# Moving adaLN filler steps along layer 0, and two elementwise steps from VectorE to ScalarE

## The chip, the cores and the metric

One core of one Trainium2 chip. The core has a matrix engine (PE in the profile, its weight loads PEld), a vector engine (DVE), a scalar engine (ACT), a general engine (POOL) and a queue for transfers (SP); they run on their own and wait for each other by semaphores. The metric is the device time of one execution of the kernel in microseconds, the median of several runs, as the slowest core shows it (here there is one).

## The reference, cut to what matters

Two layers are applied to 640 tokens of width 2048: 128 context tokens and 512 latent ones, with the same weights and two conditioning vectors. All data is in 32 bit.

```python
def layer_step(x, cvec, p, rope, attend, s0_f, s0_b):
    shift, scale, gate = adaln(cvec, w_ada, b_ada)       # silu(cvec) @ w_ada + b_ada
    h = rms_norm(x, norm_g) * (1.0 + scale) + shift
    aq, ak, av, ag, bq, bff, bfb, bi, bg, cu, cv, cg = split_proj(h @ w_in)
    q, k, v = qkv_heads(aq, ak, av, qg, kg, rope)
    a_out = attend(q, k, v) * jax.nn.silu(ag)
    b_out, s_f, s_b = hgrn_mixer(bq, bff, bfb, bi, bg, lb, hg, s0_f, s0_b)
    c_out = sgu_mixer(cu, cv, cg, lng, lnb, ws, bs)
    y = jnp.concatenate([a_out, b_out, c_out], axis=-1) @ w_out
    return x + gate * y, k, v, s_f, s_b
```

`w_ada` is 2048 x 6144 a layer: 12 column blocks of 512, of which blocks 0 to 3 give the shift, 4 to 7 the scale and 8 to 11 the gate. `attend` is a windowed softmax attention of 8 heads with a sink in the denominator; `hgrn_mixer` is a recurrence over 4 heads, run forward and backward, whose output is normalised per token and head.

## The kernel before, in words

The tokens stand as five tiles of 128 (the first is the context). Every product with `w_in` and `w_out` is taken in three matmuls on high and low parts (`wsplit`, L635 to 642: ACT rounds the weight into `wh`, DVE subtracts to get `wl`). A pass over 512 columns with tokens as rows is `rowmajor` (240 matmuls, L652 to L654, in 15 groups; the last group takes two weight tiles); a pass over 128 columns with tokens as columns is `colmajor` (96 matmuls, L660, in four groups).

Layer 0 goes through these passes: the first round and the first query pass, the second query pass, BI, CU of heads 1 to 3 and CG of head 0, then for each of four recurrence heads BFF, BFB, BQ and BG, then AG of heads 0 to 5, CV, AG of heads 6 and 7, CG of heads 1 to 3, `split_mix`, and the output projection `out_proj` in four column chunks. Layer 1 begins with `begin_next`: norm, scaling and split of its input (L586 to L624), then four row passes, then the same order, with its CU passes after CV.

Two kinds of other work are woven in. The side queue (`self.side`) holds generators of the attention (`attn`), the recurrence (`hgrn`) and the gating unit (`sgu`), moved on by `tick` at set places in each pass. The filler is a generator of adaLN blocks: each call of `fill`, one a group, adds `fill_rate` to a credit and takes one step for each whole credit.

```python
    def fill(self):
        self.credit += self.fill_rate
        while self.credit >= 1:
            self.credit -= 1
            self.step()
```

A block (`ada_steps`, L290) takes 18 steps. Each of the first 16 loads a 128 x 512 piece of `w_ada` into one of two buffers, on SP, with raised priority, and multiplies and adds it on DVE into the accumulator `aacc`, once for each conditioning vector (L300 for the first piece, L302 for the others). There is one `aacc` buffer. The 17th step is empty; the 18th sums over partitions on PE (L308 for the gate, L319 for shift and scale) and writes the result (`mod_cols`). Layer 0's queue has 12 blocks, set in `begin`: its own gate, then layer 1's shift and scale; layer 1's queue has its own gate, at rate 0.5, set after the first pass of `begin_next`. They are counted here from 0 to 11, and 12 to 15. `drain` takes all steps that are left; it is called after each layer's output projection.

The text below numbers these `fill` calls from the second query pass of layer 0 on: 15 a row pass, 4 a column pass, 169 up to `split_mix`, 60 in the output projection.

The order of instructions on each engine isn't the order of the text: a scheduler makes it, from priorities (the place in the text; `hi()` raises it by 3000) and from when inputs and buffers are free.

In `attn`, scores go through exp on ACT with the row sum as a second output (L925), then DVE adds the sink's term, takes the reciprocal (L927, L928) and multiplies the four heads' probabilities by it (L930); four ticks later PE transposes them (L941). A tile of 128 queries has 512, 384 or, for the context, 128 probabilities a head. In `hgrn`, for each of five tiles PE sums the output in a PSUM bank, ACT squares it with a row sum (L1123) and DVE copies it to `ob` (L1124); at the end DVE scales `ob` (L1137) and PE transposes it (L1143).

In `out_proj`, each chunk takes five PSUM banks; the last CG pass before it must empty its two banks first, which `mul_evac` does (exp on ACT, L1206, product on DVE, L1208, then `sigma`, L226 to L229).

Of the kernel before, what the change touches and what calls it, by code (L numbers as in the profile page):

```python
# [12 lines left out]
AF = mybir.ActivationFunctionType  # L13
ALU = mybir.AluOpType
# [4 lines left out]
P = 128  # L19
# [56 lines left out]
class Net:  # L76
# [788 lines left out]
    def attn(self, l, gi, t):  # L865
        nc = self.nc
# [7 lines left out]
        rmax, nmx, es, den = (st[:, 4 * i:4 * i + 4] for i in range(4))  # L874
        snk = self.snk[:, l, 4 * gi:4 * gi + 4]
        nsnk = self.nsnk[:, l, 4 * gi:4 * gi + 4]
        if t > 0:
# [9 lines left out]
            for h in range(4):  # L887
# [3 lines left out]
                for p0, ds, pn in pieces:  # L891
                    ks = slice(p0, p0 + ds * pn, ds)
                    so = s[:, o * P:(o + pn) * P].rearrange("p (b k) -> p b k", k=P)
                    for i, (x, y) in enumerate(((qh, kh), (qh, kl), (ql, kh))):
# [5 lines left out]
                                               op0=ALU.add, op1=ALU.max, accum_out=rmax[:, h:h + 1])  # L900
# [4 lines left out]
            dst = src  # L905
        else:
# [11 lines left out]
            dst = [m[:, h * P:h * P + P] for h in range(4)]  # L918
# [8 lines left out]
        nc.vector.tensor_tensor(den, den, es, op=ALU.add)  # L927
        nc.vector.reciprocal(den, den)  # L928
        for h in range(4):
            nc.vector.tensor_scalar(dst[h], dst[h], den[:, h:h + 1], None, op0=ALU.mult)  # L930
        yield
        yield
        yield
# [114 lines left out]
    def hgrn(self, l, h, es, q):  # L1048
        nc, I, O = self.nc, self.I, self.O
# [7 lines left out]
        for d in range(2):  # L1057
# [7 lines left out]
            for n in range(4):  # L1065
                j = order[d][n]
# [13 lines left out]
        ob = self.g()  # L1080
        ss = self.small(NT, "oss")

        def build(j):
            K = []
            for d in range(2):
                k = self.Cm[:, d, 0:512]
                dd = pre[d][3][:, j, 0:4]
                if d:
                    dd = dd[:, :, ::-1]
                nc.gpsimd.tensor_tensor(k.rearrange("p (i c s) -> p i c s", i=4, c=4),  # L1090
                                        bc(c4(pre[d][0])[:, j], 1, 4), bc(dd, 3, 32), op=ALU.mult)
                K.append(k)
            return K
# [4 lines left out]
        for n in range(NT + 3):  # L1098
            if n < NT:
                for d in range(2):  # L1100
                    qe = pre[d][1]
                    ab = self.bank()
                    for i in range(4):
                        ri = 3 - i if d else i
                        nc.tensor.matmul(ab[32 * i:32 * i + 32, 0:P], lhsT=qe[:, n * P + 32 * i:n * P + 32 * i + 32],  # L1105
                                         rhs=K[d][:, ri * P:(ri + 1) * P], start=True, stop=True,
                                         skip_group_check=True)
                    nc.vector.copy_predicated(self.att[d], self.m8[:, 1 - d], ab[:, 0:P])
                asum = self.sml.tile([P, P], F32, tag="asum", name=self.nm("asum"), bufs=2)
                nc.vector.tensor_tensor(asum, self.att[0], self.att[1], op=ALU.add)  # L1110
                sums[n] = asum
                if n + 1 < NT:
                    K = build(n + 1)
            if n >= 3:
                j = n - 3
                oo = self.bank()
                nc.tensor.matmul(oo[:, 0:P], lhsT=aTs[j], rhs=vj[j], start=True, stop=j == 0)
                if j > 0:
                    for d in range(2):
                        nc.tensor.matmul(oo[:, 0:P], lhsT=pre[d][2][:, j * P:(j + 1) * P],  # L1120
                                         rhs=S[d][:, order[d].index(j) - 1], start=False, stop=d == 1)
                junk = self.sml.tile([P, P], BF16, tag="junk", name=self.nm("junk"), bufs=1)
                nc.scalar.activation(junk, oo[:, 0:P], AF.Square, accum_out=ss[:, j:j + 1])  # L1123
                nc.vector.tensor_copy(ob[:, j * P:(j + 1) * P], oo[:, 0:P])  # L1124
            yield
            if 1 <= n <= NT:
                tb = self.bank()
                nc.tensor.transpose(tb[:, 0:P], sums.pop(n - 1), self.ident)
                aT = self.sml.tile([P, P], F32, tag="aT", name=self.nm("aT"), bufs=2)
                nc.scalar.activation(aT, tb[:, 0:P], AF.Copy)  # L1130
                aTs[n - 1] = aT
                yield
# [8 lines left out]
        for j in range(NT):  # L1141
            dst = b1[:, j * P:(j + 1) * P] if j < 4 else b2[:, 0:P]
# [128 lines left out]
    def begin(self, W):  # L1271

        with self.hi():
            self.setup()
            self.first_round(W)
            act, dve = self.second_round(W)
        with self.tc.issue_after(act), self.tc.issue_after(dve):
            self.setup2()
            self.prep_ctx(0)
        self.filler = self.ada_gen([(0, b) for b in range(8, 12)] + [(1, b) for b in range(8)])  # L1280
        self.fill_rate = 1.0
        steps = self.bias_rows(W)

        def hook(k):
            if k < 8:
                self.shift_h(k + 8)
            if k:
                next(steps, None)

        ps = self.rowmajor(W, AQ + 512, hook)  # L1290
        for _ in steps:
            pass
        self.q_evac(0, 1, ps)
# [18 lines left out]
    def layer(self, l):  # L1312
        W = self.I["w_in"][l]
        nc = self.nc
# [47 lines left out]
        if l > 0:  # L1362
            self.drain()
        self.split_mix()
        self.out_proj(l)
        self.drain()

# [56 lines left out]
```

## Time and profile before

| what | value |
|---|---|
| median of 3 runs | 2344.2 us (2340.97 to 2345.61) |
| the profiled execution's own time | 2338.18 us |
| its span, from the first to the last instruction | 2336.4 us |
| mean granted clock of PE | 0.988 |
| second query pass to CG of head 0 (layer 0) | 205.7 to 457.5 us |
| recurrence passes, layer 0 | 457.5 to 739.6 us |
| AG, CV, AG and CG passes, layer 0 | 739.6 to 998.9 us |
| output projection, layer 0 | 998.9 to 1247.9 us, with the first part of the hand-over to layer 1 |
| recurrence passes, layer 1 | 1531.6 to 1805.7 us |
| output projection, layer 1 | 2114.0 to 2331.4 us |

The stages run from the first matmul of one pass to the first of the next. In the rows of the profile a line number is that of the kernel; `x480` is a count; after the bar come busy us, mean ns of one, then the engine's idle time ahead of the group and what ended it. A busy PE is no measure by itself, since matmuls overlap; how long the same matmuls take in two stages is.

### The profile page before, as it was taken

What the parts mean: (1) busy time and instruction counts of PE and PEld (TensorE: products, weight loads), DVE (VectorE), ACT (ScalarE), POOL (GpSimd) and SP (SyncE); (2) the same over time, 40 slices, a digit from 0 to 9 for tenths busy, and PEclk for the clock granted to TensorE, in tenths of its full rate; (3) what the DMA queues carried; (4) which work ended last, traced back from release to release, by engine and by line L of the source; (5) the groups of instructions that cost most, each with busy time, mean ns of one, the idle gap of its engine ahead of it and who ended that gap; (6) DMA issues with size and microseconds to landing.
All of it is one profiled execution on the core that took longest, in us unless ns stands there. A gap on an engine that the chain in (4) does not pass through costs nothing.

```text
span 2336.4 us, 34944 instructions
## 1 busy us (share of the span) xinstructions
PE 2261.4 (97%) x13308; PEld 1968.0 (84%) x13308; DVE 1424.3 (61%) x2612; ACT 778.7 (33%) x1605; POOL 293.9 (13%) x234
## 2 busy tenths in 40 slices
PE   7999999999999989989999999999999999999999
PEld 5766678899999888977787878799999998998887
DVE  3436987768887766666667455855875942434223
ACT  3323434343334322332224234344343332223111
POOL 0000111002122211011112010101222220101110
PEclk9999999999999999999999999999999999999999
DMA  9675632434433354355552221322332323324332
GB/s 321 218 254 191 209 117 83 148 95 120 126 117 104 111 163 144 111 192 171 173 170 91 77 68 47 115 68 72 111 94 76 114 90 92 103 75 149 106 106 84
DMA packets 264876, 296.41 MB, mean 127 GB/s; under 512 B 17378, under 2 KB 166772, under 8 KB 262916
## 3 DMA queue, kind: packets, MB, share of 16 engines
q1 hardware_dynamic: 254368, 271.27, 37.2%
q10 hardware_dynamic: 10340, 22.91, 3.2%
q8 instruction: 104, 1.70, 0.3%
q14 instruction: 64, 0.52, 0.1%
HBM read 280.38 MB, written 13.73 MB: 126 GB/s over the span
## 4 chain that ended last, share of the span: by engine, by line
PE 75%; DVE 12%; DMA 7%; issue 2%; ACT 1%; POOL 0%; DVEq 0%; ACTq 0%; POOLq 0%
PE m L660 29%; PE m L652 11%; PE m L653 11%; PE m L654 11%; DMA wa<-in_w_ada_dram 6%; DVE aacc L302 4%; DVE wl L641 2%; PE s L240 2%; PE s L895 1%; PE s L941 1%; PE s L1105 1%; PE s L1072 1%; PE s L953 1%; PE s L954 1%; PE s L319 1%
## 5 line engine op out<-in xcount | busy, mean ns | idle before, releaser
L641 DVE TENSOR_TENSOR wl<-wr,wh 128x512 fp32r<-128x512 f32 (+1 forms) x535 | 401.5, 752 | 575.2 <-ACT wh L640 566.7
L640 ACT ACTIVATE wh<-wr 128x512 fp32r<-128x512 f32 (+1 forms) x535 | 336.1, 629 | 971.0 <-PE m L654 557.2
L652 PE MATMUL m<-wh,hh 128*128 128x512 f32 x1440 | 571.6, 397 | 9.2 <-DVE mg L1208 5.3
L653 PE MATMUL m<-wl,hh 128*128 128x512 f32 x1440 | 568.5, 395 | 3.5 <-DVE wl L641 3.5
L654 PE MATMUL m<-wh,hl 128*128 128x512 f32 x1440 | 565.6, 393 | 0.0
L660 PE MATMUL m<-hh,wh 128*128 128x384 f32 x2016 | 478.1, 317 | 0.0
L660 PE MATMUL m<-hl,wh 128*128 128x384 f32 x2016 | 465.0, 311 | 0.0
L660 PE MATMUL m<-hh,wl 128*128 128x384 f32 x2016 | 464.6, 311 | 0.0
L302 DVE SCALAR_TENSOR_TENSOR aacc<-wa,s,aacc 128x512 f32<-128x512 f32 x480 | 368.6, 801 | 72.9 <-DMA wa<-in_w_ada_dram 72.3
L652 PEld LDWEIGHTS m<-wh,hh 128*128 128x128 f32 x1440 | 272.0, 189 | 84.5 <-issue 10.3
L653 PEld LDWEIGHTS m<-wl,hh 128*128 128x128 f32 x1440 | 272.7, 189 | 64.2 <-DVE wl L641 7.4
L654 PEld LDWEIGHTS m<-wh,hl 128*128 128x128 f32 x1440 | 272.4, 189 | 59.0 <-issue 2.6
L660 PEld LDWEIGHTS m<-hh,wh 128*128 128x128 f32 x2016 | 312.5, 190 | 9.8 <-issue 8.1
L660 PEld LDWEIGHTS m<-hl,wh 128*128 128x128 f32 x2016 | 311.5, 189 | 0.4
L660 PEld LDWEIGHTS m<-hh,wl 128*128 128x128 f32 x2016 | 311.1, 189 | 0.3
L1090 POOL TENSOR_TENSOR mg<-ev,Dt 128x512 f32<-128x512 f32 x80 | 95.7, 1213 | 321.5 <-PE s L1105 107.2
L1260 POOL TENSOR_TENSOR mg<-mg,ev 128x512 f32<-128x512 f32 x30 | 43.9, 1473 | 287.9 <-DVE ev L1258 287.1
L751 POOL TENSOR_TENSOR mg<-g,g 128x256 f32<-128x256 f32 x32 | 32.8, 1047 | 263.8 <-DVE g L749 145.5
L925 ACT ACTIVATE g<-g,st,qs 128x384 f32<-128x384 f32 (+1 forms) x64 | 48.1, 752 | 36.0 <-DVE st L921 36.0
L228 ACT ACTIVATE ev<-ev 128x640 f32<-128x640 f32 x40 | 29.5, 738 | 72.3 <-DVE ev L227 71.2
L945 DVE TENSOR_TENSOR g<-s,g 128x512 fp32r<-128x512 f32 x56 | 38.4, 687 | 24.0 <-ACT g L944 18.1
L1045 POOL TENSOR_TENSOR g<-g,EG 128x512 f32<-128x512 f32 x16 | 22.7, 1416 | 239.4 <-DVE Dt L1030 125.1
(272 smaller groups left out, 1984.6 us busy)
## 6 DMA issues: line engine op xcount, KB each, us to landing
wr<-in_w_in_dram SPq DMA_DIRECT2D x406, 256.0 KB, 2.9
wa<-in_w_ada_dram SPq DMA_DIRECT2D x278, 256.0 KB, 3.0
wr<-in_w_out_dram SPq DMA_DIRECT2D x128, 256.0 KB, 2.9
wa<-in_w_ada_dram SPq DMA_DIRECT2D x16, 1024.0 KB, 6.7
wa<-in_w_in_dram SPq DMA_DIRECT2D x9, 1024.0 KB, 6.5
wa<-in_w_ada_dram SPq DMA_DIRECT2D x44, 128.0 KB, 3.3
mg<-const_xT_dram SPq DMA_DIRECT2D x4, 1280.0 KB, 5.8
x<-mg SPq DMA_DIRECT2D x20, 256.0 KB, 2.1
```

The costliest lines, as they stand in the source:

```text
L240: return self.nc.tensor.matmul(acc[32 * q:32 * q + 32, 0:n], lhsT=lhs[:, kk, :], rhs=rhs, start=kk < 4, stop=kk >= 12, skip_group_check=True)
L302: nc.vector.scalar_tensor_tensor(acc[:, cd], r, sc, acc[:, cd], op0=ALU.mult, op1=ALU.add)
L640: nc.scalar.activation(wh, raw, AF.Copy)
L641: nc.vector.tensor_tensor(wl, raw, wh.bitcast(F32), op=ALU.subtract)
L652: nc.tensor.matmul(ps, lhsT=hh, rhs=wh[:, 0], start=k == 0, stop=False)
L653: nc.tensor.matmul(ps, lhsT=hh, rhs=wl[:, 0], start=False, stop=False)
L654: nc.tensor.matmul(ps, lhsT=hl, rhs=wh[:, 0], start=False, stop=k == KT - 1)
L660: self.nc.tensor.matmul(ps[hf][:, 0:n], lhsT=w[:, a], rhs=h[:, o:o + n], start=k == 0 and i == 0, stop=k == KT - 1 and i == 2)
L925: nc.scalar.activation(dst[h], src[h], AF.Exp, bias=nmx[:, h:h + 1], scale=rq[:, h:h + 1], accum_out=den[:, h:h + 1])
L945: nc.vector.tensor_tensor(pt[1], pb, pt[0].bitcast(F32), op=ALU.subtract)
L1090: nc.gpsimd.tensor_tensor(k.rearrange("p (i c s) -> p i c s", i=4, c=4), bc(c4(pre[d][0])[:, j], 1, 4), bc(dd, 3, 32), op=ALU.mult)
L1260: (nc.vector if c == 3 else nc.gpsimd).tensor_tensor(xs, xs, y, op=ALU.add)
```

## The change

The filler's rate in layer 0 goes from 1.0 to 0.85, and to 1.25 when the output projection begins. The four multiplications by the reciprocal in `attn` and the copy of the output in `hgrn` become ACT instructions (`Copy`, with a per-partition scale in `attn`). Nothing else differs; layer 1's rate stays at 0.5.

```diff
@@ -927,7 +927,7 @@
         nc.vector.reciprocal(den, den)
         for h in range(4):
-            nc.vector.tensor_scalar(dst[h], dst[h], den[:, h:h + 1], None, op0=ALU.mult)
+            nc.scalar.activation(dst[h], dst[h], AF.Copy, scale=den[:, h:h + 1])
@@ -1121,7 +1121,7 @@
                 nc.scalar.activation(junk, oo[:, 0:P], AF.Square, accum_out=ss[:, j:j + 1])
-                nc.vector.tensor_copy(ob[:, j * P:(j + 1) * P], oo[:, 0:P])
+                nc.scalar.activation(ob[:, j * P:(j + 1) * P], oo[:, 0:P], AF.Copy)
@@ -1278,7 +1278,7 @@
         self.filler = self.ada_gen([(0, b) for b in range(8, 12)] + [(1, b) for b in range(8)])
-        self.fill_rate = 1.0
+        self.fill_rate = 0.85
@@ -1362,6 +1362,8 @@
         self.split_mix()
+        if l == 0:
+            self.fill_rate = 1.25
         self.out_proj(l)
         self.drain()
```

## The prediction

> **What bounds the kernel now.** First the page: its head, the engines, the chain.
>
> ```profile
> span 2336.4 us, 34944 instructions
> ...
> PE 2261.4 (97%) x13308; PEld 1968.0 (84%) x13308; DVE 1424.3 (61%) x2612; ACT 778.7 (33%) x1605; POOL 293.9 (13%) x234
> ...
> PE 75%; DVE 12%; DMA 7%; issue 2%; ACT 1%; POOL 0%; DVEq 0%; ACTq 0%; POOLq 0%
> PE m L660 29%; PE m L652 11%; PE m L653 11%; PE m L654 11%; DMA wa<-in_w_ada_dram 6%; DVE aacc L302 4%; DVE wl L641 2%; PE s L240 2%; PE s L895 1%; PE s L941 1%; PE s L1105 1%; PE s L1072 1%; PE s L953 1%; PE s L954 1%; PE s L319 1%
> ```
>
> PE sets the time: three quarters of the chain is matmuls. What can still be won are its gaps, and the chain says whose they are: 6% of it is the load of adaLN weights, 4% their multiply-add on DVE (L302). That work belongs to the filler. So the second view is busy time by stage, the third PE's waits.
>
> ```profile
> 457.50:739.60 282.10, 279.54 (x2063) 267.49 (x2062) 218.25 (x396) 107.68 (x233) 51.32 (x39) 0.99 0.38 113
> 998.90:1182.10 183.20, 172.66 (x754) 139.04 (x753) 109.76 (x159) 45.55 (x85) 25.61 (x17) 0.98 0.53 173
> 1531.60:1805.70 274.10, 272.17 (x2023) 261.96 (x2022) 170.63 (x324) 105.10 (x228) 47.84 (x39) 1.00 0.29 83
> 2114.00:2331.40 217.40, 217.40 (x962) 179.98 (x960) 67.67 (x95) 44.88 (x72) 22.96 (x17) 1.00 0.32 107
> ```
>
> Columns after the length: busy PE, PEld, DVE, ACT, POOL, then granted clock, DMA. The first and third rows are the 16 recurrence passes of layers 0 and 1: the same matmuls take 8.0 us longer in layer 0, where the filler is thicker. The other two are output projections: three column chunks of layer 0 (61.1 us each) against four of layer 1 with no filler (54.4 each). The filler costs PE 6.7 us a chunk there; DVE is busy only 60% of it.
>
> ```profile
> PE s L1143 <- DVE g L1137: 10.4, 6, 6.1
> PE s L941 <- DVE g L930: 8.7, 6, 3.2
> PE s L1072 <- ACT g L1068: 7.7, 2, 4.1
> PE m L652 <- DVE mg L1208: 5.3, 1, 5.3
> PE s L1193 <- DVE mg L1194: 5.1, 1, 5.1
> PE s L1128 <- DVE att L1108: 1.9, 1, 1.9
> ```
>
> Few and long waits (total, times, longest): single ones reach 3 to 6 us. The change can win these and little else.
>
> **When the filler runs.** Not evenly. DVE's timeline around two block starts:
>
> ```profile
> 814.51 0.17 DVE L284 TENSOR_TENSOR sh<-s,cols 128x8 f32<-128x8 f32 x1 [1.64 <-PE s L319]
> 814.60 0.48 DVE L300 TENSOR_SCALAR aacc<-wa,s 128x512 f32<-128x512 f32 x1
> ...
> 942.82 0.74 DVE L302 SCALAR_TENSOR_TENSOR aacc<-wa,s,aacc 128x512 f32<-128x512 f32 x1
> ...
> 974.39 0.17 DVE L287 SCALAR_TENSOR_TENSOR gs<-s,cols 128x8 f32<-128x8 f32 x1 [2.94 <-PE s L319]
> 974.48 0.48 DVE L300 TENSOR_SCALAR aacc<-wa,s 128x512 f32<-128x512 f32 x1
> ...
> L302 DVE SCALAR_TENSOR_TENSOR aacc<-wa,s,aacc 128x512 f32<-128x512 f32 x480 | 368.6, 801 | 72.9 <-DMA wa<-in_w_ada_dram 72.3
> ```
>
> A block (L300) starts as soon as the closing matmuls (L319) of the one before it have run, since there is one accumulator (`aacc`, bufs=1). Then its 16 steps follow in a burst (block 7 of layer 0's queue 0 to 11 from 814.60; block 8 ends at 942.82) and nothing comes until 974.48. A step is two instructions of 801 ns; a burst is 25.6 us of DVE. So the rate does not thin the bursts. It moves the closing matmuls, which stand on PE where the filler step was traced: step 18n+18 for block n.
>
> Before, that is fill call 18n+18: blocks 6 and 8 close at calls 126 and 162, the last group of pass AG3 and the first of CG2, where 814.51 and 974.39 stand. Of layer 0's calls 169 come ahead of the output projection. At 0.85, block n closes at call (18n+18)/0.85 rounded up: 22, 43, 64, 85, 106, 128, 149; then 143 steps are out, and at 1.25 blocks 7 to 11 close at calls 170, 184, 199, 213, 227. Burst n+1 follows each. By the passes' times of before, bursts 3 to 11 begin near 540, 631, 719, 823, 912, 1003, 1055, 1115, 1170. Ahead of the projection run eight bursts where nine and a half ran; in it 8 to 11, where half of 9, 10, 11 and block 12 (layer 1's first) ran. Block 12 now begins near 1228, as the projection ends.
>
> **The change part by part.** (1) *End of layer 0's mixing.* DVE, ACT and PE:
>
> ```profile
> 998.94 4.04 DVE L302 SCALAR_TENSOR_TENSOR aacc<-wa,s,aacc 128x512 f32<-128x512 f32 x4
> 1006.30 1.41 DVE L302 SCALAR_TENSOR_TENSOR aacc<-wa,s,aacc 128x512 f32<-128x512 f32 x2 [3.32 <-DMA wa<-in_w_ada_dram]
> 1007.63 0.88 DVE L1208 TENSOR_TENSOR mg<-mg,m 128x384 f32<-128x384 f32 x2
> ...
> 1000.86 0.77 ACT L1206 ACTIVATE ev<-m 128x384 f32<-128x384 f32 x2 [5.06 <-DMA mg<-in_x_sample_dram]
> ...
> 1008.20:1012.20 4.00, 3.96 (x9) 3.15 (x10) 2.99 (x6) 1.00 (x2) 0.00 (x0) 0.50 0.59 193
> ```
>
> The projection waits for a PSUM bank that L1208 must empty; burst 9 stands ahead of it, with a 3.32 us wait for a load. Afterwards PE runs 4 us at a granted clock of 0.50, which loses 2.0 more. With burst 8 starting only after the projection's first group, L1208 comes near 1002: -7.3, and burst 8's own slowing in the chunk about +2: -5.3 (between -8 and 0, if DVE's order keeps a load's wait ahead of it). The ACT queue's x load, 5.06 us, stays.
>
> (2) *Pass AG2.*
>
> ```profile
> 779.95 4.02 DVE L302 SCALAR_TENSOR_TENSOR aacc<-wa,s,aacc 128x512 f32<-128x512 f32 x4
> ...
> 780.13 0.74 ACT L228 ACTIVATE ev<-ev 128x640 f32<-128x640 f32 x1 [5.47 <-DVE ev L227]
> 782.06 0.58 ACT L1068 ACTIVATE g<-s 128x512 f32<-128x512 f32 x1
> 783.00:787.00 4.00, 4.00 (x21) 4.00 (x20) 4.00 (x6) 1.26 (x3) 0.43 (x1) 0.57 0.56 166
> ```
>
> Burst 6 holds L227, ACT's queue waits 5.47 us for that with L1068 behind it, PE loses 4.1, then 4 us at 0.57 (1.7 more). New burst 5 is over near 760, burst 6 starts near 823: take -5 of 5.8 (0 if something else holds L227). (3) The 1.9 at L1128 (near 588, old burst 4) falls between new bursts 3 and 4: -1.9. (4) The 6.1 at L1143 lies at 846, in burst 7 before and in burst 6 after; the 5.1 at L1193, at 938, in burst 8 before and 7 after: nothing won, and the other new places may hurt: +2, between -6 and +8. (5) Half a burst more in the projection, at 6.7 a chunk and about one burst a chunk: 3.4, less half of a block's closing matmuls, which only move:
>
> ```profile
> L319 PE MATMUL s<-ones,aacc 128*128 128x1 f32 x128 | 14.7, 245 | 0.0
> ```
>
> 14.7 us over eight blocks is 1.8 each, so +2.4 (0 to +5). A step moved takes its load along, 16 a block, issued on SP among the weight loads; its buffer comes free only when DVE has done the step two before, and in a burst SP therefore holds weights back. That is in the 6.7, since it is measured with it; what covers it is the four weight buffers.
>
> (6) *Block 12 in the hand-over.*
>
> ```profile
> 1228.00:1247.90 19.90, 14.36 (x63) 10.80 (x61) 16.01 (x35) 13.04 (x33) 0.00 (x0) 0.83 0.44 147
> 1247.90:1311.40 63.50, 63.50 (x309) 52.92 (x307) 36.77 (x66) 23.07 (x43) 12.87 (x8) 0.97 0.23 65
> ```
>
> DVE is free 3.9 and 26.7 us there; the burst needs 25.6 and, at the mean wait of 72.3 us over 256 steps, 4.5 for loads. The norm, scaling and split of layer 1's input are ahead of it in priority, so steps fill holes; SP's queue carries its loads among the next weights', which are four buffers deep. Bounds 0 and +17 (half the steps ahead of the split, 15.1, and 2 at half clock); I take +4.
>
> (7) *Division and copy.*
>
> ```profile
> L930 DVE TENSOR_SCALAR g<-g,st 128x512 f32<-128x512 f32 x32 | 13.8, 482 | 0.2
> L930 DVE TENSOR_SCALAR g<-g,st 128x384 f32<-128x384 f32 x32 | 11.3, 414 | 0.2
> L930 DVE TENSOR_SCALAR g<-g,st 128x128 f32<-128x128 f32 x16 | 3.5, 280 | 0.2
> L599 ACT ACTIVATE mg<-mg,rr 128x512 f32<-128x512 f32 x8 | 5.2, 709 | 0.0
> L382 ACT ACTIVATE hh<-mg,gs 128x128 fp32r<-128x128 f32 x16 | 6.3, 391 | 9.0 <-DVE gs L288 9.0
> L1124 DVE COPY g<-s 128x128 f32<-128x128 f32 x40 | 11.3, 281 | 7.5 <-ACT junk L1123 7.4
> L1130 ACT ACTIVATE aT<-s 128x128 f32<-128x128 f32 x40 | 10.9, 273 | 47.5 <-PE s L1128 47.5
> L640 ACT ACTIVATE wh<-wr 128x512 fp32r<-128x512 f32 (+1 forms) x535 | 336.1, 629 | 971.0 <-PE m L654 557.2
> ```
>
> DVE loses 13.8+11.3+3.5+11.3 = 39.9 us and 7.4 of waiting; ACT gains 32x0.709, 32x0.60 (between 709 and 391, by width), 16x0.391 and 40x0.273 = 59 us and stands at 36%. Four divisions take 0.91 (512), 0.74 (384) or 0.44 us (128) longer, and ACT now waits for the reciprocal (DVE, L928) with the weight splits L640 queued behind, DVE's L641 behind those and PE behind both. What covers that is ACT's lead: before L640 it sat idle 971.0 us, 557.2 of it until PE gave a buffer back. A wait of a few us uses the lead up; a longer one stalls PE one for one. PE waited six times for the division: +4 if each grows; against it DVE hands back 28.6 us, all in attention: -2 net, between -9 and +14 (20 tiles at 0.7 us). The copy follows the square on its own engine instead of through DVE's queue, so L1137 and L1143 come sooner: -2 of 10.4, at worst 0.
>
> Sum: -5.3 -5 -1.9 +2 +2.4 +4 -2 -2 = -7.8 us, which takes the profiled execution's 2338.2 us (span 2336.4 and 1.8 around it) to 2330.4. The median of the three runs lies 6 us above the profiled one, so 2344.2 - 7.8 gives 2336.
>
> **The rivals.** *The hand-over pays*: block 12's steps stand ahead of layer 1's split, (6) at its upper end: +13, 2349. It decides once about eight of the sixteen run before the last L617. For it: DVE's room there is nearly all used. Against it: priority, and PE's stalls there are now waits for DVE and ACT that the filler doesn't join. *Stalls only move*: the new bursts cost at other points what (1) to (3) win: 2344, give or take 4. For it: DVE's total falls by 40 us only, and every burst so far cost about 5. *ACT is the slower engine*: PE waits for each of 20 divided tiles, +14 instead of -2 in (7) at most, some +8 by half of them: 2346. The rows say 709 against 482 ns; against it only six waits are on the chain today. The Trainium skill, page "ScalarE: Activation LUTs", section "Rules for kernel authors", says just this: multiply on VectorE, not ScalarE. The rows agree per instruction; the page does not weigh which engine has room. *Attention was bound by DVE*: (7) at its low end, -9, and (4) at -6: 2321.
>
> **How the numbers follow.** Forecast 2336, 46%; hand-over 13%; moved stalls 20%; ACT 10%; attention 11%. About 0.2% (4.7 us) is what a measurement of this kernel tells from no change: faster is below 2339.5, slower above 2348.9. The forecast lies mostly in the first, the moved stalls in the middle, ACT in both of the upper. Faster 0.57, same 0.26, slower 0.17. The range leaves out the far ends: 2322 to 2349; the forecast's own is 2330 to 2342.
>
> **What would show it.** L300 starts at the nine places named; no L302 between L300 of block 8 and the CG3 L1208; the waits at L652 and L1072 (layer 0) gone; L1143 and L1193 kept; L613 and layer 1's first pass longer by some 4 us; L941's wait shared out between ACT and DVE. Wrong if bursts start elsewhere (the model of the one accumulator), or if the instruction order on DVE, made anew for the whole program, shifts stalls in layer 1's recurrence, where nothing but (7) changes.

## The result, and the profile after

Timed together, the kernel before takes 2342.59 us (median of four, 2340.47 to 2345.61) and the changed one 2330.34 us (median of four, 2327.87 to 2332.5). The ratio is 0.9946, with a 95% interval of 0.9929 to 0.9964: 0.5% faster, some 12.6 us. The ratios further down are each taken against 15 to 20 runs of the kernel before that were timed with them. The profiled execution after took 2330.76 us with a span of 2329.0, which is 7.4 below the span of before. The medians lie further apart than the spans because the profiled execution of before, 2338.18 us, was one of its quicker ones. The stages below add up to the 7.4; what the rest of the 12.6 consists of, they can't show.

The page of the changed kernel: head, engines, chain and the filler's multiply-add:

```profile
span 2329.0 us, 35021 instructions
...
PE 2257.8 (97%) x13308; PEld 1963.2 (84%) x13308; DVE 1385.8 (60%) x2492; ACT 824.9 (35%) x1725; POOL 290.4 (12%) x234
...
PE 68%; DVE 11%; DMA 6%; issue 2%; ACT 2%; POOL 0%; DVEq 0%; SPq 0%; ACTq 0%; POOLq 0%
...
L302 DVE SCALAR_TENSOR_TENSOR aacc<-wa,s,aacc 128x512 f32<-128x512 f32 x480 | 370.0, 802 | 85.5 <-DMA wa<-in_w_ada_dram 84.4
```

PE still sets the time. DVE has lost 38.5 us of busy time and ACT has gained 46.2: the division and the copy, 39.9 us on DVE before. The multiply-add costs what it did (802 ns), and its waits for loads have grown from 72.3 to 84.4 us: the filler did not become cheaper, it stands elsewhere.

Where it stands, in DVE's timeline of the changed kernel about the start of the output projection:

```profile
990.99 0.17 DVE L284 TENSOR_TENSOR sh<-s,cols 128x8 f32<-128x8 f32 x1 [2.51 <-PE s L319]
991.07 1.54 DVE L300 TENSOR_SCALAR aacc<-wa,s 128x512 f32<-128x512 f32 x2
992.53 0.87 DVE L1208 TENSOR_TENSOR mg<-mg,m 128x384 f32<-128x384 f32 x2
```

Burst 8 begins here, 4 us into the projection, and `L1208`, which empties the PSUM bank that the projection waits for, follows after the first two multiplications. Before, burst 9 stood there and `L1208` came at 1007.63.

PE's waits, changed kernel (total, times, longest):

```profile
PE s L941 <- ACT g L930: 11.2, 7, 3.8
...
PE s L1072 <- ACT g L1068: 5.7, 2, 4.6
PE s L1143 <- DVE g L1137: 5.6, 4, 2.0
PE s L608 <- issue: 5.3, 1, 5.3
PE s L1105 <- DVE att L1108: 4.4, 4, 1.8
PE s L1105 <- DVE mg L1078: 4.2, 1, 4.2
PE s L1193 <- DVE mg L1194: 3.4, 1, 3.4
PE s L613 <- DVE g L617: 2.5, 1, 2.5
```

Gone are the 5.3 us at `L652` and the 1.9 at `L1128`; `L1143` has halved and its longest fell from 6.1 to 2.0. Of the two waits at `L1072` the one in layer 0 fell from 4.1 to 1.1, the one in layer 1 grew. New are five waits at `L1105` in layer 0's recurrence and one at `L608` in the hand-over to layer 1, where the waits at `L613` fell from 5.6 us in all to 2.5. The wait for the division has not shrunk; it has changed its engine and grown from 8.7 to 11.2, and the first experiment shows that the new rates alone bring that growth.

The same stages in the two kernels, from first matmul to first matmul:

| stage | before | after | difference |
|---|---|---|---|
| second query pass and BI, layer 0 | 161.1 | 162.7 | +1.6 |
| CU1 to CG0 | 90.6 | 85.1 | -5.5 |
| recurrence passes | 282.2 | 288.4 | +6.2 |
| AG0 to AG5 | 117.4 | 108.4 | -9.0 |
| CV to CG3 | 141.9 | 137.1 | -4.8 |
| projection, chunk 0 | 65.1 | 59.3 | -5.8 |
| projection, chunks 1 and 2 | 118.2 | 115.8 | -2.4 |
| chunk 3 with the hand-over, and layer 1's first pass | 129.3 | 134.5 | +5.2 |
| layer 1: second query pass, BI, recurrence | 437.6 | 444.7 | +7.1 |
| all the rest | 793.1 | 793.1 | 0.0 |

The stages don't hold quite the same work, since matmuls of the side queue and of the filler move from one to another: CU1 to CG0 has 545 PE matmuls before and 532 after, the stage ahead of it 741 and 749. So a part of the -5.5 and of the +1.6 is work that moved.

### The profile page after: what moved, and what is told of

Same layout as the page of the kernel before. It is cut to its first block, busy times and chain, and to the rows that moved or that the text cites. A ratio compares the mean times of both kernels' runs of the same rounds, so it can differ in the third digit from the quotient of the medians.

```text
span 2329.0 us, 35021 instructions
## 1 busy us (share of the span) xinstructions
PE 2257.8 (97%) x13308; PEld 1963.2 (84%) x13308; DVE 1385.8 (60%) x2492; ACT 824.9 (35%) x1725; POOL 290.4 (12%) x234
## 4 chain that ended last, share of the span: by engine, by line
PE 68%; DVE 11%; DMA 6%; issue 2%; ACT 2%; POOL 0%; DVEq 0%; SPq 0%; ACTq 0%; POOLq 0%
PE m L660 32%; PE m L653 9%; PE m L654 9%; PE m L652 9%; DMA wa<-in_w_ada_dram 5%; DVE aacc L302 4%; DVE wl L641 2%; PE s L895 1%; PE s L941 1%; PE s L1105 1%; PE s L953 1%; DVE g L749 1%; DVE g L748 1%; PE s L954 1%; DMA wr<-in_w_in_dram 1%
## 5 line engine op out<-in xcount | busy, mean ns | idle before, releaser
L641 DVE TENSOR_TENSOR wl<-wr,wh 128x512 fp32r<-128x512 f32 (+1 forms) x535 | 395.8, 742 | 585.9 <-ACT wh L640 578.6
L652 PE MATMUL m<-wh,hh 128*128 128x512 f32 x1440 | 572.6, 398 | 2.4 <-ACT hh L382 2.1
L653 PE MATMUL m<-wl,hh 128*128 128x512 f32 x1440 | 569.3, 395 | 2.8 <-DVE wl L641 2.5
L302 DVE SCALAR_TENSOR_TENSOR aacc<-wa,s,aacc 128x512 f32<-128x512 f32 x480 | 370.0, 802 | 85.5 <-DMA wa<-in_w_ada_dram 84.4
L652 PEld LDWEIGHTS m<-wh,hh 128*128 128x128 f32 x1440 | 272.1, 189 | 76.8 <-issue 10.5
L653 PEld LDWEIGHTS m<-wl,hh 128*128 128x128 f32 x1440 | 272.6, 189 | 63.1 <-DVE wl L641 7.5
L1090 POOL TENSOR_TENSOR mg<-ev,Dt 128x512 f32<-128x512 f32 x80 | 103.1, 1304 | 327.5 <-PE s L1105 113.3
L941 PE MATMUL s<-misc,g 128*128 128x128 f32 x240 | 45.6, 286 | 11.5 <-ACT g L930 11.2
```

The lines of the kernel that those rows point to most:

```text
L302: nc.vector.scalar_tensor_tensor(acc[:, cd], r, sc, acc[:, cd], op0=ALU.mult, op1=ALU.add)
L641: nc.vector.tensor_tensor(wl, raw, wh.bitcast(F32), op=ALU.subtract)
L652: nc.tensor.matmul(ps, lhsT=hh, rhs=wh[:, 0], start=k == 0, stop=False)
L653: nc.tensor.matmul(ps, lhsT=hh, rhs=wl[:, 0], start=False, stop=False)
L941: nc.tensor.transpose(pb[:, h * P:(h + 1) * P], dst[h][:, kb * P:(kb + 1) * P], self.ident)
```

## The experiments

The theory to be tested: what the change wins comes from where the bursts of the filler stand, and the division and the copy win a little more. The rivals: the engine change does it, the stalls merely move, or the rate matters as a rate (fewer steps where DVE is scarce).

**The change taken apart.** Each edit is made to the kernel before. Only the rates:

```diff
-        self.fill_rate = 1.0
+        self.fill_rate = 0.85
...
+        if l == 0:
+            self.fill_rate = 1.25
```

> The two rates alone (0.85, then 1.25); division and copy stay on DVE. Theory A (the gain is the filler's bursts leaving the points where PE waited on DVE): 10 us faster than before, some 2332, with bursts beginning at the same places as in the changed kernel (345, 440, 538, 633, 723, 824, 910, 991 us), the wait of L652 for L1208 gone and the output projection's first three chunks some 8 us shorter. Theory B (the gain is DVE's relief by 40 us): 0 to 4 us faster. Theory C (the scheduler makes a new order for the whole program, and the parts don't add): anything, with layer 1's stages changed too although nothing of theirs was edited.

Measured: 2330.58 us, ratio 0.9959 (0.9948 to 0.9971), as theory A has it. The rates alone make most of the gain, and as far as the intervals tell perhaps all of it. The bursts began within 11 us of the places named, and the wait of `L652` for `L1208` fell to 0.2 us. By stages, which are those of the slowest of its five runs, the recurrence became 15.2 us longer, more than in the full change, and the second query pass with BI 5.1, against 8.0 less in CU1 to CG0, 8.3 less in AG0 to AG5, 5.1 less in CV to CG3 and 7.5 less in the first three chunks (8 foretold); the hand-over paid 4.9, and layer 1 behind its first pass kept its times within 0.3. PE's wait for the division, which is still on DVE here:

```profile
PE s L941 <- DVE g L930: 11.4, 6, 3.8
```

That is the 11.2 of the changed kernel. So in the changed kernel this wait grew with the places of the bursts, and not because ACT does the division.

Only the division, and only the copy:

```diff
-            nc.vector.tensor_scalar(dst[h], dst[h], den[:, h:h + 1], None, op0=ALU.mult)
+            nc.scalar.activation(dst[h], dst[h], AF.Copy, scale=den[:, h:h + 1])
```

> The softmax division alone on ACT. Theory A: between 5 us faster and 5 us slower; L941's wait moves from DVE to ACT, 8.7 us before and some 10 to 12 us after, and layer 1's attention passes (second query pass to the first recurrence passes) get some 5 us longer, as they did in the changed kernel. Theory B: 5 to 9 us faster, both layers' attention shorter.

```diff
-                nc.vector.tensor_copy(ob[:, j * P:(j + 1) * P], oo[:, 0:P])
+                nc.scalar.activation(ob[:, j * P:(j + 1) * P], oo[:, 0:P], AF.Copy)
```

> The copy of the recurrence's output alone on ACT. Theory A: 0 to 3 us faster; the wait of L1143 for L1137 falls from 10.4 us towards 6, most of it at the one long wait in pass AG5 (6.1 us) if that one came from two passes through DVE's queue; it stays at 6 there if it came from the filler burst alone. Theory B: 3 to 5 us faster.

Measured: 2347.58 us, ratio 1.0025 (1.0014 to 1.0035), and 2344.51 us, ratio 1.0021 (1.001 to 1.0031). Either alone makes the kernel slower, by 0.2%. For the division the expectation had room for that, and the wait at `L941` is as foretold; layer 1's attention and recurrence grew by 2.8 us where 5 was foretold. For the copy it failed: 0 to 3 us faster was foretold, with the waits at `L1143` falling towards 6 us, and they grew to 15.1. PE's waits with the division alone:

```profile
PE s L1143 <- DVE g L1137: 12.5, 6, 8.1
PE s L941 <- ACT g L930: 10.3, 5, 3.3
```

The longest wait at `L1143` stands in pass AG5. DVE's multiply-adds ahead of `L1137` there, in the kernel before and then with the division alone:

```profile
840.86 4.01 DVE L302 SCALAR_TENSOR_TENSOR aacc<-wa,s,aacc 128x512 f32<-128x512 f32 x4 [0.94 <-DMA wa<-in_w_ada_dram]
...
846.26 1.06 DVE L1137 TENSOR_SCALAR g<-g,oss 128x128 f32<-128x128 f32 x5
```

```profile
847.50 3.35 DVE L302 SCALAR_TENSOR_TENSOR aacc<-wa,s,aacc 128x512 f32<-128x512 f32 x4 [2.50 <-DMA wa<-in_w_ada_dram]
...
852.31 0.75 DVE L302 SCALAR_TENSOR_TENSOR aacc<-wa,s,aacc 128x512 f32<-128x512 f32 x1 [0.66 <-DMA wa<-in_w_ada_dram]
852.98 1.07 DVE L1137 TENSOR_SCALAR g<-g,oss 128x128 f32<-128x128 f32 x5
```

The order is the same in both: four multiply-adds, a weight split (`L641`), a copy (`L1124`), one more multiply-add, which in the kernel before waits for no load. What grew are the waits for loads, from 0.94 to 3.16 us, and with them PE's wait, from 6.1 to 8.1. DVE's timeline with the copy alone in the same pass, and ACT's last step ahead of `L1137`:

```profile
845.41 3.25 DVE L302 SCALAR_TENSOR_TENSOR aacc<-wa,s,aacc 128x512 f32<-128x512 f32 x4 [2.60 <-DMA wa<-in_w_ada_dram]
...
850.25 1.41 DVE L302 SCALAR_TENSOR_TENSOR aacc<-wa,s,aacc 128x512 f32<-128x512 f32 x2 [0.98 <-DMA wa<-in_w_ada_dram]
851.58 0.67 DVE L1137 TENSOR_SCALAR g<-g,oss 128x128 f32<-128x128 f32 x3
...
844.90 0.21 ACT L1134 ACTIVATE oss<-oss 128x5 f32<-128x5 f32 x1
```

The copies were done on ACT by 844.7, and the factors of `L1137` by 845.1. Yet `L1137` comes at 851.58: six multiply-adds are ahead of it, one more than before, and 2.60 and 0.98 us of their waits for loads, where before had 0.94. PE's wait at `L1143` grew from 6.1 to 8.0 us there. This is the cost that "the copy follows the square on its own engine" left out: DVE does its instructions in one order, and a load that is late for one holds all behind it. Why the loads came later in both runs wasn't followed.

Rates and copy, with the division on DVE:

```diff
-                nc.vector.tensor_copy(ob[:, j * P:(j + 1) * P], oo[:, 0:P])
+                nc.scalar.activation(ob[:, j * P:(j + 1) * P], oo[:, 0:P], AF.Copy)
...
-        self.fill_rate = 1.0
+        self.fill_rate = 0.85
...
+        if l == 0:
+            self.fill_rate = 1.25
```

> Rates and copy, with the division back on DVE: the changed kernel less one part. Theory A: as fast as the changed kernel or up to 5 us faster (2326 to 2332), since the division gave layer 1 some 7 us and took some 4 from layer 0. Theory B: 6 us or more slower than the changed kernel (2337 or above).

Measured: 2329.25 us, ratio 0.9952 (0.9939 to 0.9965). It lies in the range foretold by theory A, 2326 to 2332. The three kernels with the new rates, 0.9959, 0.9952 and 0.9946, can't be told apart by their intervals. So the two engine changes, which cost 0.2% each at the old places of the bursts, cost or win nothing that shows at the new ones.

Layer 1 grew by 7.1 us in stages where the text of the kernel differs by the division and the copy alone. To see whether the division is to blame, the changed kernel with layer 1's division back on DVE:

```diff
+            if l == 0:
                 nc.scalar.activation(dst[h], dst[h], AF.Copy, scale=den[:, h:h + 1])
+            else:
+                nc.vector.tensor_scalar(dst[h], dst[h], den[:, h:h + 1], None, op0=ALU.mult)
```

> The changed kernel with layer 1's softmax division back on DVE, layer 0's still on ACT. Theory A: layer 1's passes from the second query pass to the end of the recurrence, 444.7 us in the changed kernel against 437.7 before, come back to about 438: some 5 us faster than the changed kernel, 0.992 to 0.993 of before. Theory C (the order is made anew each time and the parts don't add): anywhere within 6 us of the changed kernel, layer 0 changed too.

Measured: 2328.34 us, ratio 0.9943 (0.9931 to 0.9956); the stages took 442.1 us where 438 was expected and 444.7 stood. A third of the loss came back, and nothing of it shows in the time. Over all runs of this study these stages take 440.5 to 444.7 us in the five kernels with layer 1's division on ACT, and 437.3 to 442.1 in the nine without; 441.4 is the run with the filler put off by 8 calls (below), in which neither layer 1's division nor its copy was touched. So the division may have some of the 7.1 us, but up to 4 of such a loss come with a new order of the program alone, and no run tells the two apart.

**Place or rate?** If the place of the bursts is what counts, another way to move them should do as well. The kernel before, at rate 1.0 all through, with the credit starting below zero, so that all bursts come later by that many fill calls:

```diff
         self.fill_rate = 1.0
+        self.credit = -8.0
```

> The kernel before, at rate 1.0 throughout, with the filler's start put off by 8 calls (credit begins at -8) and nothing else changed: the same number of filler steps in each pass, nine bursts ahead of the projection, but each 8 calls later. Block closings at calls 26, 44, 62, 80, 98, 116, 134, 152, 170, 188, 206, 224, so bursts begin near 609 (block 4), 764 (6), 855 (7), 921 (8) and 991 (9) us. Theory A1 (what counts is where the bursts stand): the 5.3 us wait of L652 for L1208 and the 6.1 us wait at L1143 in pass AG5 go, the waits at L1072 in AG2 and L1193 in AG7 stay, the hand-over gets 4 us longer; 5 to 11 us faster than before. Theory A2 (what counts is that fewer bursts run ahead of the projection): within 3 us of before.

Measured: 2327.58 us, ratio 0.9945 (0.9931 to 0.9958). One line that changes neither a rate nor an engine wins all that the change wins, and theory A2 (within 3 us of before) falls. The gain therefore comes with moving the bursts; a rate below 1 isn't needed for it. But which stalls would go was foretold badly. The bursts began within 11 us of the places named, and yet the waits at `L1072` in AG2 and `L1193` in AG7, which were to stay, are gone too (these passes take 15.8 and 18.6 us against 21.3 and 27.1), while the recurrence takes 12.6 us more, with 12.4 us of new waits at `L1105`. Whether a place is good in itself or by the order that the scheduler makes for it, no run separates.

Two more offsets, to see whether the places named in the prediction can foretell a kernel's time:

```diff
+        self.credit = -4.0
```

> As the run with the start put off by 8 calls, but by 4. Closings at calls 22, 40, 58, 76, 94, 112, 130, 148, 166, 184, 202, 220: burst 9 begins in the last CG pass (near 988 us), ahead of the L1208 on which the projection waits, burst 7 near 832 and so over the L1143 of pass AG5, burst 8 near 903 and so over the L1193 of AG7. Theory A1 (place alone): most long waits of before stay, within 5 us of before (0.998 to 1.002). Theory A2' (any delay of the filler helps, in proportion): half of what 8 calls gave, 0.997.

```diff
+        self.credit = -12.0
```

> The same, put off by 12 calls. Closings at 30, 48, 66, 84, 102, 120, 138, 156, 174, 192, 210, 228: burst 7 lies in CV, 8 begins after AG7's L1193, 9 in the first chunk of the projection, 11 across the end of the third chunk, and block 12 wholly in the hand-over. Theory A1: the waits at L1143 of AG5, L1193 and L652 go, the hand-over costs 5 us: 6 to 12 us faster than before, 0.995 to 0.9975. Theory A2': 1.5 times what 8 calls gave, 0.992.

Measured: 2324.49 us, ratio 0.9931 (0.9915 to 0.9946), and 2332.91 us, ratio 0.9966 (0.9956 to 0.9976). The second came as expected. The first did not, by either theory: it is the fastest kernel of the study, though its bursts stand on places at which I had seen long waits. It alone has a shorter recurrence than before, 278.1 us against 282.2 (288.4 in the changed kernel). PE's waits at offset 4:

```profile
PE s L1143 <- DVE g L1137: 5.3, 4, 2.1
PE s L1193 <- DVE mg L1194: 4.1, 1, 4.1
```

The waits at `L1143` and `L1193` are there, but `L1143`'s longest is 2.1 and not 6.1. So "a burst stands on this pass" tells that a wait is possible; how long it is depends on how many multiply-adds still stand ahead of the instruction that PE needs, and on whether their loads have come. That changed with every edit here. Over the offsets 0, 4, 8 and 12 the ratio goes 1, 0.9931, 0.9945, 0.9966: offset 0, the kernel before, is the worst of the four, and there is no slope to follow.

**The projection.** The changed kernel with less and with more filler in it:

```diff
-            self.fill_rate = 1.25
+            self.fill_rate = 0.85
```

> The changed kernel without its second rate: 0.85 in the output projection too. By the count of calls 22 of the 216 steps (the end of block 10 and all of block 11) are left when the projection ends, and drain takes them there, with layer 1's scaling waiting for block 11. Both theories: slower than the changed kernel, by 25 to 50 us; a step with its load took 2.3 to 2.8 us in the bursts, and what PE does meanwhile is the tail of the last chunk only. If the loss is under 10 us, the model of the steps' places on PE is wrong.

Measured: 2370.97 us, ratio 1.0129 (1.0113 to 1.0145). PE's waits:

```profile
PE s L319 <- DVE aacc L302: 33.9, 1, 33.9
```

What isn't done by the end of the projection is drained in one piece, with PE idle for 33.9 us; the run is some 40 us slower than the changed kernel, where 25 to 50 was foretold. The rate of 1.25 is there to avoid this. It earns nothing in the first two chunks, which take 57.9 and 56.2 us at 0.85 and 59.3 and 58.2 at 1.25.

```diff
-            self.fill_rate = 1.25
+            self.fill_rate = 1.5
```

> The changed kernel with 1.5 in place of 1.25 in the output projection. Block 11 closes at the 49th group of the projection instead of the 58th, so that block 12's burst runs inside the last chunk and not into the hand-over to layer 1. Theory A (the hand-over costs because that burst stands among the norm and scaling on DVE): the last chunk with the hand-over comes back from 70.2 to about 66 us, the rest as in the changed kernel: 3 to 5 us faster than it, 0.992 to 0.993 of before. Rival (denser bursts in the projection cost as much as they save, or the hand-over is long for another reason): the same time as the changed kernel, 0.9946, with longer waits of L653 for L641 in the chunks.

Measured: 2344.0 us, ratio 1.0016 (1.0007 to 1.0025): the whole gain is lost. I had expected the hand-over to become cheaper, and its wait at `L608` did go. But all four chunks became longer: 4.4, 3.0, 2.8 and 4.9 us. PE's waits in the projection, kernel with 1.5:

```profile
PE m L652 <- DVE ev L1258: 6.0, 5, 2.2
...
PE m L653 <- DVE wl L641: 4.2, 3, 2.0
...
PE s L319 <- DVE aacc L302: 2.4, 2, 2.2
```

The changed kernel has 2.5 us at `L653` there and nothing in the other two rows, so these waits hold 10 of the 15 us.

`L1258` empties the PSUM banks of a chunk that has ended, for the next one. DVE's timeline at such a chunk's end, kernel with 1.5:

```profile
1112.90 0.68 DVE L1258 TENSOR_TENSOR ev<-m,g 128x512 f32<-128x512 f32 x1
1113.50 1.18 DVE L302 SCALAR_TENSOR_TENSOR aacc<-wa,s,aacc 128x512 f32<-128x512 f32 x1
1114.60 0.68 DVE L1258 TENSOR_TENSOR ev<-m,g 128x512 f32<-128x512 f32 x1
```

and the changed kernel at the same place:

```profile
1098.95 0.69 DVE L1258 TENSOR_TENSOR ev<-m,g 128x512 f32<-128x512 f32 x1 [0.67 <-PE m L654]
```

In the first DVE is the one that is waited for, with a multiply-add between two evacuations; in the second DVE waits for PE. At 1.25 a block's 18 steps take 14.4 groups and a chunk has 15, so a burst begins as a chunk begins and is nearly over when it ends.

How much hangs on this can be read from stretches of 13 us about the ends of chunks 0, 1 and 2 (8 ahead, 5 behind; of before those of 0 and 1), with the multiply-adds alone (busy DVE and their number; clock, DMA share, GB/s). The kernel before, then offset 4, then the one with 1.5, then the one with 0.85:

```profile
1055.90:1068.90 13.00, 7.50 (x8) 1.00 0.56 182
1116.00:1129.00 13.00, 4.37 (x5) 1.00 0.50 164
```

```profile
1038.80:1051.80 13.00, 1.40 (x2) 1.00 0.49 154
1095.00:1108.00 13.00, 0.00 (x0) 1.00 0.42 145
1151.20:1164.20 13.00, 0.00 (x0) 1.00 0.54 183
```

```profile
1044.60:1057.60 13.00, 4.88 (x5) 1.00 0.50 170
1105.80:1118.80 13.00, 7.05 (x7) 1.00 0.61 205
1166.20:1179.20 13.00, 7.50 (x9) 1.00 0.52 171
```

```profile
1041.90:1054.90 13.00, 0.00 (x0) 1.00 0.53 187
1098.10:1111.10 13.00, 7.47 (x10) 1.00 0.50 164
1160.00:1173.00 13.00, 5.97 (x7) 1.00 0.60 199
```

Chunk 1 of before, between 8 and 5 of them, took 60.1 us with 11.5 steps in it; chunks 1 and 2 of offset 4, with hardly any at their ends, took 56.2 each with 16 steps; chunk 1 at rate 1.5, between 5 and 7, took 61.2 with 21. (Steps are counted from the instructions of `L300` and `L302`, two a step.) A chunk without filler takes 54.4. The run with 0.85 separates place from amount, and shows which end pays: its chunk 1, with 13 steps, none about its start and ten multiply-adds about its end, took 56.2; its chunk 2, with 7 steps, but those ten about its start, took 61.9. So a whole burst inside a chunk can cost as little as 1.8 us, and filler over the change from one chunk to the next costs the next one 5.4 to 7.5 (5.4 is chunk 2 of offset 12, with nine about its start). It isn't the whole of it: chunk 1 of offset 8, with a whole burst, no multiply-add about its start and only two about its end, took 58.0, and chunk 1 of the changed kernel, with two about its start, 58.2, which is 3.8 over the empty one. This is read from several kernels side by side; no run moved a single burst and nothing else.

**The hand-over.** In the changed kernel block 12 begins at 1210.6, and its steps stand between the last evacuations:

```profile
1215.36 0.75 DVE L302 SCALAR_TENSOR_TENSOR aacc<-wa,s,aacc 128x512 f32<-128x512 f32 x1
1216.02 0.69 DVE L1258 TENSOR_TENSOR ev<-m,g 128x512 f32<-128x512 f32 x1
```

If that is what costs 5.2 us, holding the first multiplication of a block back until layer 1's input has been scaled should win it. Tried on the changed kernel and on offset 8:

```diff
-            nc.vector.tensor_scalar(h[:, P:T], b, self.gs[:, l, k, 1:2], ...
+            x = nc.vector.tensor_scalar(h[:, P:T], b, self.gs[:, l, k, 1:2], ...
...
+            self.hold = x.ins
...
+                    with ExitStack() as st:
+                        if self.hold is not None:
+                            st.enter_context(self.tc.issue_after(self.hold))
+                        nc.vector.tensor_scalar(acc[:, cd], r, sc, None, op0=ALU.mult)
```

> The changed kernel with block 12's first multiplications queued on DVE behind the last scaling of layer 1's input (an order on DVE alone, no new wait on another engine). Theory A (the hand-over is long because that burst's steps stand among the last chunk's evacuation and the norm): the last chunk with the hand-over comes back from 70.2 us to about 66, the first pass of layer 1 stays near 64 or gains up to 3, and the whole is 3 to 5 us faster than the changed kernel, 0.992 to 0.993 of before. Rival (the hand-over is long since the order there differs for another reason, such as the norms of all five tiles taken together): no change against the changed kernel.

> The filler's start put off by 8 calls at rate 1.0, with the same hold on block 12; division and copy on DVE. Theory A: the hand-over, 72.3 us in the run with the start put off, comes back to 66 to 68: 0.991 to 0.993 of before, the fastest so far. Rival as above: 0.9945, as without the hold.

Measured: 2330.87 us, ratio 0.9953 (0.9939 to 0.9967), and 2327.99 us, ratio 0.9946 (0.9931 to 0.9961): no gain over 0.9946 and 0.9945, as the rival has it. The wait at `L608` is gone in the first, the waits at `L613` are back at 6.0 us in all (5.6 before the change), and PE waits more for the weights, changed kernel with the hold (its lines are numbered four higher, so these are `L653` for `L641`):

```profile
PE m L657 <- DVE wl L645: 5.2, 7, 1.7
```

against 2.5 us in five waits without the hold. The stage, taken apart at the projection's last matmul, shows that theory A holds for a part:

| | before | changed | changed, with hold |
|---|---|---|---|
| the 240 matmuls of chunk 3 | 56.4 | 58.8 | 59.8 |
| from there to layer 1's first pass | 9.4 | 11.5 | 9.4 |
| layer 1's first two passes | 120.2 | 121.0 | 124.4 |

The hold gave back the 2.1 us in the middle row; these were block 12's. It lost more in the passes behind, where the held burst runs now (1254.9 to 1291.7). And the chunk itself stays long with no step of block 12 in it: burst 11 stands over its start. Offset 8 with the hold has three steps in this chunk, but nine multiplications and multiply-adds about its start, and its 240 matmuls take 62.0 us; the kernel before and offset 4 have 16 steps in it, none about its start, and take 56.4.

**Not tried.** A second `aacc` buffer would let a block's first multiplication run before the closing matmuls of the one before, and might so take the bursts apart. Whether there is room for it, and whether it pays, no run shows.

## Why the prediction was right, and where it was wrong

The sign and the main reason were right: the bursts moved as the model has it, and that brings the gain, with the engine change or without. That the sum, -7.8, meets the -7.4 of the profiled spans is luck. The terms (3), (4) and (5) were some 13 us too dear, (6) and (7) some 12 too cheap if layer 1's 7.1 is set against (7), and the errors cancelled. The measured gain is larger, 12.6 us with an interval of 8.4 to 16.6. So the median, 2330.3, lies 5.7 under the 2336 foretold, at the lower edge of the forecast's own range. Of that 1.6 us are the base, whose median over four runs is 2342.6 and not 2344.2. The rest can't be assigned to stages, since these come from one execution each, and that of the kernel before lay 4.4 us under its median.

- **The model of the bursts** held. Bursts 3 to 11 were foretold near 540, 631, 719, 823, 912, 1003, 1055, 1115, 1170 and came at 538.5, 633.2, 722.8, 824.5, 910.2, 991.1, 1047.8, 1105.7, 1155.4. The later ones are early because the program is: the projection begins 12 us sooner, its last chunk 20. Against the chunks they came later than foretold: bursts 9 and 10 were put 9 us ahead of the ends of chunks 0 and 1, and began 1.5 and 1.2 us after them, inside the next chunk. This was not foreseen, and by the section on the projection it is a cheap place. Block 12 came at 1210.6 instead of 1228, 2.7 us later against its chunk. That `L1208` comes ahead of burst 8's multiply-adds is as foretold. One reading of before was off by a step: block 8's last multiply-add begins at 944.86, not 942.82.
- **(1) End of the mixing:** -5.3 foretold; chunk 0 lost 5.8, and its granted clock (the column after POOL) is 1.00 all through, without the 4 us at 0.50:

```profile
987.10:1046.30 59.20, 58.67 (x274) 48.25 (x273) 42.09 (x63) 18.29 (x33) 7.40 (x6) 1.00 0.62 206
```

 But the x load on ACT's queue, 5.06 us, "stays", it said, and it did not: `L1206` now waits 0.55 us for PE and for no load, since of the two loads of x that stood ahead of it one is now issued 9 us behind it. ACT, changed kernel:

```profile
987.14 0.77 ACT L1206 ACTIVATE ev<-m 128x384 f32<-128x384 f32 x2 [0.55 <-PE m L660]
...
995.97 0.33 ACTq L1244 DMA_DIRECT2D mg<-in_x_sample_dram  x1
```

- **(2) Pass AG2:** -5 foretold; it went from 21.3 to 16.8 us, -4.5. A wait of 1.1 us at `L1072` is left.
- **(3) and (4), the other stalls of layer 0:** this step failed in both directions. The 1.9 at `L1128` went, but burst 3 now stands on pass BQ1 of the recurrence, with a new wait of PE:

```profile
574.64 0.69 PE L1105 MATMUL s<-mg,g 128*32 128x128 f32 x16 [4.19 <-DVE mg L1078]
```

 The recurrence grew by 6.2 us where I had +2 for all new places. Against that the passes with the waits at `L1143` and `L1193`, "nothing won", won 7.0 (AG5, 24.0 to 17.0) and 3.3 (AG7, 27.1 to 23.8), though bursts 6 and 7 stand there as foretold. In AG5 of the changed kernel DVE does, with ACT's last step ahead of `L1137` below,

```profile
835.36 2.73 DVE L302 SCALAR_TENSOR_TENSOR aacc<-wa,s,aacc 128x512 f32<-128x512 f32 x4
...
840.85 1.42 DVE L302 SCALAR_TENSOR_TENSOR aacc<-wa,s,aacc 128x512 f32<-128x512 f32 x2 [2.15 <-DMA wa<-in_w_ada_dram]
842.18 0.67 DVE L1137 TENSOR_SCALAR g<-g,oss 128x128 f32<-128x128 f32 x3
...
839.61 0.21 ACT L1134 ACTIVATE oss<-oss 128x5 f32<-128x5 f32 x1
```

 It is the order of the run with the copy alone, six multiply-adds with one split between them. But their first four had their loads and had run by 838.1, before the factors of `L1137` were there at 839.8, so that only two were left to wait for. With the copy alone the same four waited 2.60 us for a load and began after those factors. PE waited 1.4 us here, and 8.0 there. I judged a stall by whether a burst stands on it; the runs show that its size is set by how much of the burst is still to come when PE's instruction could go, and by the loads that this rest waits for. All together, from CU1 to CG3 without AG2, layer 0 won 8.6 us where the terms (3) and (4) gave +0.1. Of it 5.5 lie in CU1 to CG0, which no term from (1) to (6) named.
- **(5) More filler in the projection:** +2.4 foretold; chunks 1 and 2 became 2.4 shorter. The price was mis-sized: 6.7 us a chunk was the mean of three chunks, of which the first held the wait of step (1), so that this wait was counted twice, and the other two had eight and five multiply-adds about their starts. A burst inside a chunk measures 1.8 to 3.8.
- **(6) The hand-over:** +4 foretold; +5.2 measured, 4.4 in the stage and 0.8 in the pass after it. The size is right, the place in half: 2.1 lie in the hand-over, and 2.4 in chunk 3's own matmuls, where the sum had nothing. The rival by which the hand-over pays 17 did not come about: it decides once eight of the 16 steps run ahead of the last `L617`, and four did. At offset 8 eight and a half did, and the two stages grew by 6.4.
- **(7) Division and copy:** this step is wrong. -4 foretold in all; alone they are slower by 0.25% and 0.21%, beside the new rates the time stays the same, and layer 1, where nothing else was edited, grew by 7.1 us, a part of which the runs can't put down to them. I counted the instructions that leave DVE; what counted was how long those that stay had to wait for the filler's loads, and the new order of the whole. On the price of one instruction it was right, 709 ns foretold. The division in the changed kernel at full width:

```profile
L930 ACT ACTIVATE g<-g,st 128x512 f32<-128x512 f32 x32 | 21.2, 713 | 5.3 <-DVE st L928 5.3
```

 DVE took 482 ns. PE's wait for it, 11.2 us instead of 8.7, is no mark of this price, since the new rates alone have 11.4. The Trainium skill, page "ScalarE: Activation LUTs", section "Rules for kernel authors", would have such a multiplication on VectorE; the prices and the sign of the run with the division alone agree, and beside the new rates no difference shows. The prediction named as a sign of being wrong that stalls shift in layer 1's recurrence, and it is what happened: 274.1 to 278.1 us there.

Of the rivals, "stalls only move" has some of the truth: in the recurrence and in layer 1 they did, and the AG passes and the projection paid for it. "Attention was bound by DVE" falls with the division alone, "ACT is the slower engine" has the sign of that run and not its reason alone, since 2.0 of the some 6 us were lost at the longest wait of `L1143`, to loads that DVE waited for.

One reading of the prediction was loose: its rows for the two recurrences aren't the same matmuls, but 2063 against 2023, so that a part of the 8.0 us between them is work.

The fastest kernel is offset 4, the one before with the credit starting at -4: 0.9931 (0.9915 to 0.9946), against 0.9946 (0.9929 to 0.9964) for the changed one, so that only the point is better, the intervals overlap. Still open is why its waits came out short where those of before are long; the order of DVE's instructions and the arrival of the loads can be read from a trace, but no run set either by itself.

## What to carry to other kernels

Work that is woven in step by step, but closes through a single accumulator, comes in bursts, and a rate or an offset moves the bursts rather than thins them; find where they begin and keep them off the points where buffers change hands, here the change from one chunk to the next. Try a few offsets on the chip before moving work between engines: here one line of offset wins as much as rates and engines together. An instruction taken off a busy engine pays only if what PE waits for comes sooner on that engine, so look at what stands ahead of that instruction, and at the loads which that waits for, and not at the sum of busy time.

## What the runs showed that was not expected

Moving 40 copies of 281 ns off DVE, with nothing else changed, made the kernel slower by 0.21% (0.10 to 0.31%): the order of the whole program is made anew, and such a reshuffle can be worth as much as an edit. A burst of 25.6 us of DVE cost PE 1.8 to 3.8 us where it lay inside a chunk of the projection; eight to ten multiply-adds over the change of chunks, where PSUM banks must be emptied, came with 5.4 to 7.5 us in the next chunk, even where that had few steps of its own.
